# A four-layer trunk on eight cores: reworked order, norms, pooling, convolution, weight layout and tail

## The chip, the cores and the metric

The kernel runs on the 8 cores of one Trainium2 chip, each core on one sequence of the batch, with its own copy of all weights in HBM. The time is the device time of the slowest core in microseconds (us). Cores 0 to 3 and 4 to 7 are the two dies. Some executions fall in a slow state, in which a die shows a lower granted TensorE clock; only fast runs are compared here unless I say otherwise. "Granted clock" is the share of full TensorE clock that the records of a trace show.

## The reference

`x` is (8, 2048, 1024) in FP32. Four layers follow each other; each adds a token mixer and then a squared-ReLU MLP to the residual `x`.

```python
for i in range(4):
    h = rmsnorm(x, norm_mix[i])
    if i % 3 == 0:    # mixer A (layers 0 and 3): gelu(h @ w_in) -> u, v; layernorm(v);
                      # causal mixing of v inside 128 tokens, 8 groups; (u * gate) @ w_out
    elif i % 3 == 1:  # mixer B (layer 1): p = h @ w_in; trailing means over 2, 4, 8, 16 tokens
                      # minus p; a map per group; @ w_out
    else:             # mixer C (layer 2): GLU; causal depthwise conv of 31 taps; layernorm; silu; @ w_out
    x = x + y
    x = x + square(relu(rmsnorm(x, norm_mlp[i]) @ m_w1[i])) @ m_w2[i]      # hidden 4096
return rmsnorm(x, norm_final)
```

## The kernel before

Everything is kept transposed (channels on partitions, `xT`), in four token tiles of 512. Matmuls are BF16 and add up in eight PSUM banks (TensorE's output memory); in this program a bank takes new matmuls only when the engine that reads it is done. Weights come from HBM through a ring of five 1 MB slots and are cast from FP32 to BF16 by the DMA; mixer A loads all its weights once per token tile. A helper records every operation with an estimated cost, and a list scheduler then fixes the order of each engine's instructions from these costs. That order is static: an instruction whose input is late stops everything behind it on its engine.

```python
def c_pool(n=512):                 # the scheduler's estimate for GpSimd
    return 0.15 + n / 500.0

def load_w(src_ap, view, after=()):     # src: rows of a row-major matrix, 512 (or 256) columns wide
    ...
def rms(tt, dst=None):
    # 8x square on ScalarE; 7 sums on GpSimd into sacc/acc; one FP32 matmul with 1/D;
    # sqrt on ScalarE; reciprocal on VectorE
    sum_squares(tt, acc1[:], acc1_r)
    sc.op("pe", MM(bk.v(), onesr[:], acc1[:], True, True), ..., tag="rms")
    sc.op("act", I("activation", out=dst[0], in_=bk.v(), func=AF.Sqrt, ...), table="sqrt")
    sc.op("dve", I("reciprocal", out=dst[0], in_=dst[0]), cost=3.3)

# mixer A, per token tile                        # MLP, per block fb of 512 hidden units and tile
V(tt)            # v = gelu, statistics           W1(i + 1)
ST(tt)           # layernorm of v                 W2(i)   # 8 x (4 matmuls, 1 VectorE add into xT)
self.norm(tt+1)  # norm of the NEXT tile          # after the last block: the next layer's norm
USP(tt)          # u, spatial mixing, gate
WO(tt)           # 24 matmuls, add into xT

# mixer B: window sums by doubling; groups 0..2 on VectorE, group 3 (the longest) on GpSimd
# mixer C: conv taps (128x1536 products) half on VectorE, half on GpSimd
# start: all of x is queued on one DMA queue, the gating weights of mixer A behind it
```

Of the kernel before, what the change touches and what calls it, by code (L numbers as in the profile page):

```python
# [21 lines left out]
CK = 31  # L22

# [142 lines left out]
class Op:  # L166
    __slots__ = ("i", "eng", "fns", "deps", "cost", "dma", "nbytes", "banks", "table", "users", "left",
                 "ready", "start", "end", "pos", "val", "know", "tag")


class Sched:
# [16 lines left out]
    def op(self, eng, fns, rd=(), wr=(), cost=0.1, dma=None, nbytes=0, table=None, after=(), tag=""):  # L188
        if not isinstance(fns, (list, tuple)):
            fns = [fns]  # L190
        o = Op()
        o.i, o.eng, o.fns, o.cost, o.dma, o.nbytes, o.table, o.tag = len(self.ops), eng, fns, cost, dma, nbytes, table, tag
        deps = set(after)
        banks = []
        for r in rd:
            assert not r.dead, tag
            deps |= r.w
        for r in wr:
            assert not r.dead, tag
            deps |= r.used()  # L200
        for r in rd:
            r.r.add(o.i)
        for r in wr:
            r.w = {o.i}
            r.r = set()
            r.subs = []
        for r in list(rd) + list(wr):
            if isinstance(r, Bank) and r not in banks:
                banks.append(r)
                r.refs.append(o.i)  # L210
        deps.discard(o.i)
        o.deps, o.banks = deps, banks
        self.ops.append(o)
        return o.i

    def schedule(self):
# [15 lines left out]
        table = [None]  # L232
        dma_free = 0.0
        bank_avail = {b: (0.0, ()) for b in range(self.NB)}
# [13 lines left out]
        while done < n:  # L248
            best = None
            for e in self.ENGS:  # L250
# [4 lines left out]
                for i in avail[e]:  # L255
# [3 lines left out]
                    if nb:  # L259
# [9 lines left out]
                        if len(fr) < len(nb) or (old >= self.RESERVE and len(fr) < len(nb) + self.RESERVE):  # L269
                            continue  # L270
                        rt = max(rt, fr[len(nb) - 1])
                    cand.append((max(rt, t0), i))
# [25 lines left out]
            free[e] = s + cost  # L298
            if o.dma is not None:
# [20 lines left out]
    def emit(self, block, banks):  # L320
# [52 lines left out]
        def play(eng):  # L373
            def body(e):
                for lst, o in plan[eng]:
                    for k, v in lst:
                        e.wait_ge(sems[k], v)
                    for f in o.fns[:-1]:
# [30 lines left out]
def c_pool(n=512):  # L409
    return 0.15 + n / 500.0  # L410
# [10 lines left out]
def build_program(S, layers, final):  # L421
# [15 lines left out]
    if 0 in kinds:  # L437
        din("a_w_in", (2, D, 2 * AW))
# [3 lines left out]
        din("a_w_out", (2, AW, D))  # L442
    if 1 in kinds:
        din("b_w_in", (1, D, D))
        din("b_w_grpT", (1, 4, 256, 256))
        din("b_w_out", (1, D, D))
    if 2 in kinds:
        assert S == 2048
        din("c_w_in", (1, 4, D, 512))
        din("c_taps", (4, 128, 32 * 48))  # L450
        din("c_b_dw", (D,))
        din("c_w_out", (1, D, D))
        x_spill = nc.dram_tensor("x_spill", [NT, 128, 5, 512], F32, kind="Internal").ap()
    if layers:
        din("m_w1", (4, D, HID))
        din("m_w2", (4, HID, D))
# [4 lines left out]
    uid = [0]  # L461

    def place(name, shape, dt, off, nres):
        uid[0] += 1
        size = int(np.prod(shape[1:])) * DSIZE[dt]
        assert off % 32 == 0 and off + size <= top, (name, off + size - top)
        t = nc.alloc_sbuf_tensor_at(f"{name}_{uid[0]}", list(shape), dt, offset=off)
# [10 lines left out]
    xr = lambda kc, tt: x_r[kc * NT + tt]  # L478
# [7 lines left out]
    onesf, (onesf_res,) = pers("onesf", (128, 128), F32)  # L486
    epst, (eps_res,) = pers("epst", (128, 1), F32)
    sqb = [pers(f"sq{i}", (128, 512), F32) for i in range(NSQ)]
# [14 lines left out]
    ring_n = [0]  # L503

# [5 lines left out]
    def load_w(src_ap, view, after=()):  # L510
        a, b = view
        t, r, key = take_slot()
        dst = t[:, 0:a * b].rearrange("p (a b) -> p a b", a=a)
        sc.op("pool", I("dma_start", out=dst, in_=src_ap, max_dma_last_dim=8192), wr=[r], cost=0.95,
              dma=key, nbytes=128 * a * b * 4, after=after, tag="load")
        return dst, r

    def wmat(name, idx, k0, nk, c0, nc_):

        return dram[name][idx, k0 * 128:(k0 + nk) * 128, c0:c0 + nc_].rearrange("(kc p) f -> p kc f", p=128)  # L520
# [7 lines left out]
    for tt in range(NT):  # L528
        for q in range(4):
            o = sp_dma(f"x{tt}_{q}", xT[:, 2 * q:2 * q + 2, tt * 512:(tt + 1) * 512], dram["x"][tt, :, 2 * q:2 * q + 2, :],  # L530
                       wr=[xr(2 * q, tt), xr(2 * q + 1, tt)], nbytes=128 * 4096, after=first_x[-1:] if tt else ())
            if tt == 0:
                first_x.append(o)
    sc.op("dve", I("memset", onesf[:], 1.0), wr=[onesf_res])
    sc.op("dve", I("tensor_scalar", out=onesr[:], in0=onesf[:], scalar1=1.0 / D, scalar2=None, op0=ALU.mult),
          rd=[onesf_res], wr=[onesr_res])
    sc.op("dve", I("memset", epst[:], EPS), wr=[eps_res])

# [3 lines left out]
    def sum_squares(tt, acc, acc_r):  # L542

        for kc in range(KC):
            if kc == 0:
                sq, sq_r = sacc, sacc_r
            else:
                sq, (sq_r,) = sqb[sqn[0] % NSQ]
                sqn[0] += 1
            sc.op("act", I("activation", out=sq[:], in_=xs(kc, tt), func=AF.Square),  # L550
                  rd=[xr(kc, tt)], wr=[sq_r], cost=c_act(), tag="sq")
            if kc:
                last = kc == KC - 1
                sc.op("pool", I("tensor_tensor", out=acc if last else sacc[:], in0=sacc[:], in1=sq[:], op=ALU.add),
                      rd=[sq_r, sacc_r] if last else [sq_r], wr=[acc_r if last else sacc_r], cost=c_pool(), tag="sqadd")

    def rms(tt, dst=None):

        if dst is None:
            t, (r,) = rsb[rbn[0] % 2]  # L560
            rbn[0] += 1
            dst = (t[:], r)
        sum_squares(tt, acc1[:], acc1_r)
        bk = Bank()
        sc.op("pe", MM(bk.v(), onesr[:], acc1[:], True, True), rd=[acc1_r, onesr_res], wr=[bk], cost=c_pe(1), tag="rms")
        sc.op("act", I("activation", out=dst[0], in_=bk.v(), func=AF.Sqrt, bias=epst[:, 0:1], scale=1.0),
              rd=[bk, eps_res], wr=[dst[1]], cost=c_act(), table="sqrt", tag="rsq")
        sc.op("dve", I("reciprocal", out=dst[0], in_=dst[0]), wr=[dst[1]], cost=3.3, tag="rec")
        return dst

    def rmsnorm(tt, gcol, hT, hr):
        rs, rs_r = rms(tt)
        for kc in range(KC):
            sc.op("dve", I("scalar_tensor_tensor", out=hT[:, kc, :], in0=xs(kc, tt),
                           scalar=pv[:, gcol + kc:gcol + kc + 1], in1=rs, op0=ALU.mult, op1=ALU.mult),
                  rd=[xr(kc, tt), rs_r, pv_res], wr=[hr[kc]], cost=c_dve(), tag="hT")

    def add_to_x(dc, tt, bk):
        sc.op("dve", I("tensor_tensor", out=xs(dc, tt), in0=bk.v(), in1=xs(dc, tt), op=ALU.add),
              rd=[bk], wr=[xr(dc, tt)], cost=c_dve(), tag="xadd")  # L580
# [4 lines left out]
    def mlp(l, after_tile):  # L585
        gcol = PCOLS[f"norm_mlp{l}"]
        hT = [zone(f"mh{tt}", (128, KC, 512), BF16, 8 * KB * tt, KC) for tt in range(NT)]
        aT, rl, rst, w = [], [], [], {}
        n = 8 * NT

        def prep(tt):
            h, hr = hT[tt]
            rst.append(zone(f"mrs{tt}", (128, 512), F32, 46 * KB + 2 * KB * tt))
            for kc in range(KC):
                sc.op("dve", I("tensor_scalar", out=h[:, kc, :], in0=xs(kc, tt), scalar1=pv[:, gcol + kc:gcol + kc + 1],
                               scalar2=None, op0=ALU.mult), rd=[xr(kc, tt), pv_res], wr=[hr[kc]], cost=c_dve(512, 1.4), tag="mh")
            rms(tt, (rst[tt][0][:], rst[tt][1][0]))

        def W1(i):
            fb, tt = divmod(i, NT)  # L600
            if fb == 0:
                prep(tt)
            if i == 0:
                aT.extend(zone(f"aT{j}", (128, 4, 512), BF16, 32 * KB + 4 * KB * j, 4) for j in range(2))
                rl.extend(zone(f"rl{j}", (128, 512), F32, 40 * KB + 2 * KB * j) for j in range(3))
            if tt == 0:
                w[fb] = (load_w(wmat("m_w1", l, 0, 8, fb * 512, 512), (8, 512)),
                         load_w(wmat("m_w2", l, fb * 4, 4, 0, 1024), (4, 1024)))
            wa, wr_ = w[fb][0]
            a, ar = aT[i % 2]  # L610
            h, hr = hT[tt]
            for fc in range(4):
# [3 lines left out]
                r, (rr,) = rl[(i * 4 + fc) % 3]  # L616
# [5 lines left out]
        def W2(i):  # L622
            fb, tt = divmod(i, NT)
            wb, wr_ = w[fb][1]
            a, ar = aT[i % 2]
            for dc in range(KC):
                bk = Bank()
                sc.op("pe", [MM(bk.v(), wb[:, fc, dc * 128:(dc + 1) * 128], a[:, fc, :], fc == 0, fc == 3)
                             for fc in range(4)], rd=[wr_] + ar, wr=[bk], cost=c_pe(4), tag="W2")
                add_to_x(dc, tt, bk)  # L630
            if fb == 7:
                after_tile(tt)

        W1(0)
        for i in range(n):
            if i + 1 < n:
                W1(i + 1)
            W2(i)

    class MixA:  # L640
# [6 lines left out]
        def norm(self, tt):  # L647
            self.h[tt] = mix_h(tt)
            rmsnorm(tt, self.gcol, *self.h[tt])

        def after_tile(self, tt):
            if tt < 2:
# [25 lines left out]
        def body(self, first):  # L678
            ia, h = self.ia, self.h
            if first:  # L680
                self.norm(0)
            v, v_r = zone("a_v", (128, 4, AW), BF16, 0, 24)
            vr = lambda c, vp: v_r[c * 6 + vp]
            bvb, (bv_r,) = zone("a_bvb", (128, AW), BF16, 24 * KB)
            st, st_r = zone("a_st", (128, 4, 6, 6), F32, SM_OFF + 14 * KB, 24)
            sm, sm_r = zone("a_sm", (128, 4, 4), F32, SM_OFF + 14 * KB + 576, 4)
            sc.op("pool", I("dma_start", out=bvb[:], in_=dram["a_bv"][ia].partition_broadcast(128), max_dma_last_dim=8192),
                  wr=[bv_r], cost=0.95, dma=sc.dma_key(f"a_bv{ia}"), nbytes=128 * 4 * AW,
                  after=first_x[-1:] if first else (), tag="bv")

            def V(tt):
                hT, hr = h[tt]
                for vp in range(6):
                    wv, wvr = load_w(wmat("a_w_in", ia, 0, 8, AW + vp * 512, 512), (8, 512),
                                     after=first_x[1:2] if first and tt == 0 else ())
                    for c in range(4):
                        bk = Bank()
                        sc.op("pe", [MM(bk.v(), hT[:, kc, c * 128:(c + 1) * 128], wv[:, kc, :], kc == 0, kc == KC - 1)
# [524 lines left out]
```

## Time and profile before

| | us |
|---|---|
| three runs at first | 3412.93, 3418.42, 3989.4 |
| the profiled execution, by core | 6789.2 to 8748.3 |

The execution that was profiled was slow. These lines are the head of its page and its 40 slices; a digit is a tenth.

```profile
span 8748.3 us, 45371 instructions; the slowest of 8 cores (6789.2 to 8748.3 us)
PE 8645.4 (99%) x15640; PEld 2691.2 (31%) x15640; DVE 2240.3 (26%) x3222; ACT 925.1 (11%) x1460; POOL 645.6 (7%) x572
...
PEclk9999999833333333333333333333333344444444
...
PE 99%; DVE 1%; issue 0%; POOL 0%; DMA 0%; ACT 0%; DVEq 0%; SPq 0%; POOLq 0%; ACTq 0%
```

The page says "TensorE, 99%", which is true of this execution and useless for the change: at a third of the clock TensorE hides every wait. What such a profile still gives are durations of the other engines, counts, and the few gaps that stay open even then. These are the longest waits of TensorE on its fastest core (engine, what it waited for, us in total, times, longest):

```profile
PE bank L159 <- POOL acc_57 L159: 35.7, 3, 24.5
PE bank L159 <- DVE hT_19_61 L159: 15.5, 1, 15.5
PE bank L159 <- DVE c_z_104_147 L159: 15.0, 1, 15.0
PE bank L159 <- DVE c_h_125 L159: 12.2, 1, 12.2
PE bank L159 <- DVE mh_110_153 L159: 5.5, 1, 5.5
```

They point at the start, mixer C and the MLP after it.

### The profile page before, as it was taken

The page shows a single profiled execution, that of the slowest core. Times are in us where ns is not written, and L with a number is a line of the kernel's source. Part 1 is how long each engine was busy: PE and PEld are TensorE (multiplying, and loading weights), DVE is VectorE, ACT ScalarE, POOL GpSimd, SP SyncE. Part 2 cuts the span into 40 slices and gives each one's busy share as a digit, 9 for nine tenths or more (in the row PEclk, how much of TensorE's full clock was granted, in tenths as well). Part 3 has the DMA queues.
Part 4 walks back from the last instruction along what each step waited for, and adds up shares of the span by engine and source line. Part 5 has one row for each costly group of instructions (what it writes and reads, how often), then busy time and mean ns, then how long its engine had stood idle before and what let it go on. Part 6 is the DMA issues. An engine that isn't in the chain of part 4 may idle for free.

```text
span 8748.3 us, 45371 instructions; the slowest of 8 cores (6789.2 to 8748.3 us)
## 1 busy us (share of the span) xinstructions
PE 8645.4 (99%) x15640; PEld 2691.2 (31%) x15640; DVE 2240.3 (26%) x3222; ACT 925.1 (11%) x1460; POOL 645.6 (7%) x572
## 2 busy tenths in 40 slices
PE   8999999999999999999999999999999999999998
PEld 2323232232222222222223432222223233333332
DVE  2212020222222244222223233222232123332224
ACT  1101010110000011100001111000011011110001
POOL 2000000010000022000002101000010011010001
PEclk9999999833333333333333333333333344444444
DMA  5232322230000021000001111000013444430101
GB/s 100 30 46 30 46 34 41 42 50 10 15 15 15 12 44 20 10 15 15 15 7 40 17 34 24 15 15 15 15 23 47 59 63 63 69 47 15 20 15 39
DMA packets 283438, 271.49 MB, mean 31 GB/s; under 512 B 4944, under 2 KB 251856, under 8 KB 283216
## 3 DMA queue, kind: packets, MB, share of 16 engines
q0 software_dynamic: 268144, 238.57, 18.4%
q1 hardware_dynamic: 15072, 30.02, 1.0%
q8 instruction: 133, 2.18, 0.1%
q14 instruction: 89, 0.73, 0.0%
HBM read 493.49 MB, written 13.63 MB: 58 GB/s over the span
## 4 chain that ended last, share of the span: by engine, by line
PE 99%; DVE 1%; issue 0%; POOL 0%; DMA 0%; ACT 0%; DVEq 0%; SPq 0%; POOLq 0%; ACTq 0%
PE bank L159 99%; DVE xT_43 L159 0%; DVE hT_19_61 L159 0%; DVE c_h_125 L159 0%; POOL sacc_56 L159 0%; DVE rs_16_58 L159 0%; POOL c_T_97_140 L159 0%; DMA xT_43<-x 0%; DVE c_z_104_147 L159 0%; DVE rs_17_59 L159 0%; DVE c_st_128 L159 0%; POOL acc_57 L159 0%; DVE mh_110_153 L159 0%; DVE c_mv_129 L159 0%; ACT rs_16_58 L159 0%
## 5 line engine op out<-in xcount | busy, mean ns | idle before, releaser
L159 DVE TENSOR_TENSOR xT_43<-bank,xT_43 128x512 f32<-128x512 f32 x1120 | 772.8, 691 | 2547.3 <-PE bank L159 2547.3
L159 DVE SCALAR_TENSOR_TENSOR bank<-bank,pv_49,a_S_66 128x512 f32<-128x512 f32 x96 | 72.2, 758 | 459.7 <-PE bank L159 459.3
L159 DVE TENSOR_TENSOR bank<-bank,a_bvb_63 128x512 f32<-128x512 f32 x96 | 67.2, 700 | 472.7 <-PE bank L159 463.2
L159 PE MATMUL bank<-a_uT_70,ring_6_48 128*128 128x512 bf16 x192 | 149.1, 1038 | 0.0
L159 PE MATMUL bank<-a_uT_70,ring_4_46 128*128 128x512 bf16 x192 | 148.9, 1038 | 0.0
L159 PE MATMUL bank<-a_uT_70,ring_5_47 128*128 128x512 bf16 x192 | 148.8, 1036 | 0.0
L159 DVE SCALAR_TENSOR_TENSOR bank<-bank,pv_49,a_S_149 128x512 f32<-128x512 f32 x96 | 71.8, 757 | 259.6 <-PE bank L159 259.6
L159 DVE TENSOR_TENSOR bank<-bank,a_bvb_169 128x512 f32<-128x512 f32 x96 | 67.2, 700 | 248.2 <-PE bank L159 248.2
L159 ACT ACTIVATE a_v_62<-bank 128x512 bf16<-128x512 f32 x96 | 56.8, 599 | 659.8 <-DVE bank L159 659.8
L159 ACT ACTIVATE a_uT_70<-bank,pv_49 128x512 bf16<-128x512 f32 x96 | 66.2, 689 | 539.8 <-PE bank L159 539.8
L159 POOL TENSOR_TENSOR sacc_56<-sacc_56,sq_13_55 128x512 f32<-128x512 f32 x72 | 93.3, 1296 | 285.1 <-ACT sq_13_55 L159 267.6
L159 ACT ACTIVATE a_v_168<-bank 128x512 bf16<-128x512 f32 x96 | 57.4, 598 | 479.9 <-DVE bank L159 479.9
L159 POOL TENSOR_TENSOR sacc_56<-sacc_56,sq_11_53 128x512 f32<-128x512 f32 x72 | 93.1, 1292 | 157.4 <-ACT sq_11_53 L159 137.6
L159 ACT ACTIVATE a_uT_172<-bank,pv_49 128x512 bf16<-128x512 f32 x96 | 66.2, 690 | 345.8 <-PE bank L159 345.7
L159 POOL TENSOR_TENSOR sacc_56<-sacc_56,sq_12_54 128x512 f32<-128x512 f32 x72 | 92.5, 1285 | 131.9 <-ACT sq_12_54 L159 96.0
L159 PEld LDWEIGHTS bank<-a_wmb_67,a_v_62 128*128 128x128 bf16 x384 | 71.8, 207 | 92.8 <-issue 88.7
L159 PE MATMUL bank<-a_uT_172,ring_3_45 128*128 128x512 bf16 x192 | 97.5, 720 | 0.0
L159 PE MATMUL bank<-a_uT_172,ring_2_44 128*128 128x512 bf16 x192 | 97.5, 722 | 0.0
L159 PE MATMUL bank<-a_uT_172,ring_6_48 128*128 128x512 bf16 x192 | 97.5, 720 | 0.0
L159 PE MATMUL bank<-a_wmb_67,a_v_62 128*128 128x128 bf16 x384 | 95.0, 461 | 0.0
L159 ACT ACT_TABLE_LOAD x45 | 57.7, 1283 | 327.2 <-PE bank L159 274.0
L159 PE MATMUL bank<-ring_6_48,c_h_125 128*128 128x512 bf16 x128 | 76.4, 833 | 12.2 <-DVE c_h_125 L159 12.2
(805 smaller groups left out, 12835.8 us busy)
## 6 DMA issues: line engine op xcount, KB each, us to landing
ring_2_44<-a_w_in POOLq DMA_DIRECT2D x20, 1024.0 KB, 8.1
ring_3_45<-a_w_in POOLq DMA_DIRECT2D x20, 1024.0 KB, 8.3
ring_4_46<-a_w_in POOLq DMA_DIRECT2D x20, 1024.0 KB, 8.3
ring_5_47<-a_w_in POOLq DMA_DIRECT2D x20, 1024.0 KB, 8.2
ring_6_48<-a_w_in POOLq DMA_DIRECT2D x16, 1024.0 KB, 8.2
ring_4_46<-m_w POOLq DMA_DIRECT2D x14, 1024.0 KB, 8.4
ring_2_44<-m_w POOLq DMA_DIRECT2D x13, 1024.0 KB, 8.3
ring_3_45<-m_w POOLq DMA_DIRECT2D x13, 1024.0 KB, 8.4
```

Of the source, the lines that this page charges most:

```text
L159: return lambda e: getattr(e, _method)(*[_r(a) for a in args], **{k: _r(v) for k, v in kwargs.items()})
```

## The change

Its intent is to take away every wait of TensorE. Its title names four parts (last two MLP blocks added jointly, conv taps built on GpSimd, last conv channels in two parts, tail in three parts), but it reworks all layers. The diff, cut to its core:

```diff
 # scheduler: costs, shared port, bank reservation; activation tables loaded by hand
-    return 0.15 + n / 500.0
+    return 0.2 + n / 400.0
+                    if o.port:      # VectorE and GpSimd not at once on the shared port
+                        rt = max(rt, port_free["pool" if e == "dve" else "dve"])
-                        if len(fr) < len(nb) or (old >= self.RESERVE and len(fr) < len(nb) + self.RESERVE):
+                        if len(fr) < len(nb) + old:
 # weights laid out slot by slot
-        din("a_w_in", (2, D, 2 * AW))
+        din("a_w_in", (2, 12, 128, 4096))       # and all others
 # norms: Ln and Exp on ScalarE in place of Sqrt and reciprocal; sums on GpSimd, VectorE or TensorE
+        if mode == "pe":                        # 8 FP32 matmuls add the squares up
+                sc.op("pe", MM(bk.v(...), onesr[:], sq[:, cs], kc == 0, kc == KC - 1), ...)
+    inv_sqrt: Ln(x + eps), Exp(-0.5 .)
 # start: first matmuls on x * g without the norm; x of later tiles loaded later
+                raw[0] = (hraw, hraw_r)
+                load_x(tt + 1, (cj // 4,), [last_load[0]])
 # mixer A: where the next tile's norm stands
                 ST(tt)
-                if tt + 1 < NT and h[tt + 1] is None:
-                    self.norm(tt + 1)
                 USP(tt)
+                if tt + 1 < NT:
+                    self.norm(tt + 1, after=[late_u[0]])
 # mixer B: all four groups as running sums on VectorE
-                        sc.op(eng, I("tensor_tensor", out=dst..., in0=src..., in1=src[shifted], op=ALU.add), ...)
+                        sc.op("dve", I("tensor_tensor_scan", ..., op0=ALU.add, op1=ALU.subtract), ...)
 # MLP: blocks 6 and 7 in one PSUM accumulation
+                    W2((6, 7), tt)
 # tail: last tile in three column parts
+                    cuts = ((0, 256), (256, 384), (384, 512))
 # mixer C: scaling of x on ScalarE, taps mostly on GpSimd and ahead, last channels in two parts
+                built[(i, j)] = taps(*units[i][j], *cms[Q], "dve" if j % 4 == 3 else "pool")
+            stages = [(0, 0, 256), (1, 0, 256), (2, 0, 256), (3, 0, 128), (3, 128, 128)]
```

## The prediction

> **What bounds the kernel now.** The timed runs (3413, 3418 us, and one of 3989) are not what the profile shows: the profiled execution took 6789 to 8748 us. In it 512-column matmuls start every 0.443 us at best, up to 0.84, also where the windows print a clock of 1.00, so those records are incomplete. TensorE is 98 to 99% of the chain of waits and hides almost everything. The trace counts 14,112 matmuls of 512 columns and 1,408 of 128. At the warm intervals that the Trainium skill states (TensorE: Matmul & The Clock Gate, "Wait — 56ns, not 53.3ns?": 215.7 and 55.6 ns; no run here shows them) I estimate 3,122 us, about 3,145 with the FP32 norm matmuls. That leaves some 275 us of 3418 in which TensorE waits. Only these can go.
>
> **Where they are, by estimate.**
> - Start: first matmul at 40.7 us (chain): x, seven GpSimd adds of 1.27, a 3.35 us reciprocal, eight normed tiles at 1.35. About 40.
> - Tail: the chain's last 26 us hold no matmul; with the sums before it about 35.
> - Mixer A's weights. A packet of 512 B takes 60 ns, 1,024 B 98, 2,048 B 173 (DMA records). One token tile needs 12 MB in 1,024 B and 6 MB in 512 B packets, over 16 engines about 122 us; TensorE at full clock needs 130. Contention and the ring of five buffers should stall each of eight tiles by 5 to 15 us, together with the LayerNorm between V and U. About 90.
> - Mixer B: VectorE. Its sums took 1.26 us alone, 3.0 to 3.3 beside GpSimd's; about 35.
> - Mixer C and the MLP after it: even throttled, TensorE waits 12.2 us on c_h, 15.0 on c_z, 5.5 on mh; unthrottled about 60.
>
> **What the change does.** Weights laid out slot by slot give long packets (from the three times above 22 ns plus 0.074 per byte: 18 MB in some 95 us): DMA leaves the path, −60. Start on unnormalised x: −24. Tail in three parts, squares summed on TensorE: −24. Pooling as scans on VectorE, GpSimd quiet: −25. Mixer C in finer stages: −30. Ln/Exp in place of square root and reciprocal: mostly hidden. Joint last MLP blocks save 96 VectorE additions of 0.69 us, off the path: 0 to −5. Added: FP32 sums of squares on TensorE for some nine tiles, 63 matmuls at 0.86 us at half clock, so about 0.43: +27, partly hidden in waits; scheduling by corrected costs: −5 to −15.
>
> Sum: about −160: **3255 us**, range 3195 to 3325. Faster by over 2%: 0.87; within 2%: 0.10; slower: 0.03.
>
> **What would show each step right.** Packets mostly above 4 KB, DMA share down by a fifth or more; first V matmul near 16 us; last matmul to end under 12 us; no GpSimd sums and no 3 us VectorE sums in mixer B; conv taps on GpSimd at 3.1 us, no wait of TensorE on them; 96 fewer additions into x; more FP32 matmuls. If the profile is throttled again, its span will scarcely change, and only start, tail and mixer C are to be read from it.
>
> **What would make it wrong.** If mixer A was not DMA-bound at full clock, only some 100 us are won (3310). If a denser TensorE draws a lower clock, or fast executions become rare, the gain is lost. If GpSimd taps and VectorE block each other in mixer C, its share is small.

## The result, and the profile after

| us | all runs | fast runs |
|---|---|---|
| before | 3412.93, 3418.42, 3441.86, 3989.4 | the first three |
| after | 3253.8, 3257.32, 3259.36, 3773.51 | the first three |

The ratio of the fast runs is 0.9511, 95% interval 0.9441 to 0.958: 4.9% faster. A ratio here is the mean of one kernel's fast runs over the mean of the other's in the same rounds, so it is not quite the ratio of the medians that are quoted.

The profile after fell in the fast state. First its head, slices, chain, and the same kind of waits as above (the longest of them).

```profile
span 3252.2 us, 46091 instructions; the slowest of 8 cores (3246.7 to 3252.2 us)
PE 3190.4 (98%) x16113; PEld 1533.5 (47%) x16113; DVE 1943.1 (60%) x3053; ACT 967.9 (30%) x1595; POOL 535.7 (16%) x568
...
PEclk9999999999999999999899999999999999999999
...
PE 94%; DMA 2%; issue 1%; DVE 1%; POOL 1%; ACT 0%; SPq 0%; DVEq 0%; POOLq 0%; ACTq 0%
```

```profile
PE bank L161 <- POOL c_acc L161: 14.8, 1, 14.8
PE bank L161 <- DMA a_brow<-a_bv: 3.9, 1, 3.9
PE bank L161 <- DVE a_vv_184 L161: 3.5, 4, 0.9
PE bank L161 <- ACT c_z_163 L161: 3.1, 1, 3.1
```

The waits on VectorE's `hT`, `c_h` and `mh` are gone (1.0 us is left on ScalarE's `c_h`) and that on `c_z` fell to 3.1 us; one long wait is left, on `c_acc`, and it is new. But these lines cannot be set against the throttled ones: a fast profile of the kernel before is needed. That is the first experiment.

### The profile page after: what moved, and what is told of

Same layout as the page of the kernel before. It is cut to its first block, busy times and chain, and to the rows that moved or that the text cites. A ratio compares the mean times of both kernels' runs of the same rounds, so it can differ in the third digit from the quotient of the medians.

```text
span 3252.2 us, 46091 instructions; the slowest of 8 cores (3246.7 to 3252.2 us)
## 1 busy us (share of the span) xinstructions
PE 3190.4 (98%) x16113; PEld 1533.5 (47%) x16113; DVE 1943.1 (60%) x3053; ACT 967.9 (30%) x1595; POOL 535.7 (16%) x568
## 3 DMA queue, kind: packets, MB, share of 16 engines
q0 software_dynamic: 66320, 237.79, 45.3%
## 4 chain that ended last, share of the span: by engine, by line
PE 94%; DMA 2%; issue 1%; DVE 1%; POOL 1%; ACT 0%; SPq 0%; DVEq 0%; POOLq 0%; ACTq 0%
PE bank L161 94%; DMA ring_45<-a_w_in 1%; DMA ring_47<-b_w_out 0%; DMA xT<-x 0%; DMA x_spill<-xT 0%; DVE xT L161 0%; POOL a_smv_187 L161 0%; DVE a_vv_184 L161 0%; POOL a_sm L161 0%; POOL sacc L161 0%; DVE a_v L161 0%; DVE a_S L161 0%; POOL ring_47 L161 0%; POOL c_ls L161 0%; DVE b_w_111 L161 0%
## 5 line engine op out<-in xcount | busy, mean ns | idle before, releaser
L161 DVE TENSOR_TENSOR xT<-bank,xT 128x512 f32<-128x512 f32 (+2 forms) x1040 | 706.5, 683 | 481.6 <-PE bank L161 471.4
L161 ACT ACTIVATE a_uTv_188<-bank,pv 128x512 bf16<-128x512 f32 x96 | 65.9, 686 | 100.5 <-PE bank L161 100.4
L161 ACT ACTIVATE a_uT<-bank,pv 128x512 bf16<-128x512 f32 x96 | 65.3, 686 | 100.0 <-PE bank L161 96.9
L161 DVE SCALAR_TENSOR_TENSOR bank<-bank,pv,a_Sv_165 128x512 f32<-128x512 f32 x96 | 72.0, 758 | 27.0 <-PE bank L161 26.8
L161 DVE SCALAR_TENSOR_TENSOR bank<-bank,pv,a_S 128x512 f32<-128x512 f32 x96 | 71.7, 757 | 24.8 <-PE bank L161 24.6
L161 DVE BATCH_NORM_STATS2 a_stv_186<-a_vv_184 128x6 f32<-128x512 bf16 x96 | 65.6, 687 | 25.3 <-ACT a_vv_184 L161 25.3
L161 POOL TENSOR_TENSOR sacc<-sacc,sq_57 128x512 f32<-128x512 f32 x52 | 66.8, 1284 | 80.4 <-ACT sq_57 L161 71.6
L161 DVE TENSOR_TENSOR bank<-bank,a_bvbv_185 128x512 f32<-128x512 f32 x96 | 66.1, 688 | 17.8 <-PE bank L161 17.8
L161 POOL TENSOR_TENSOR sacc<-sacc,sq_59 128x512 f32<-128x512 f32 x52 | 66.0, 1270 | 61.6 <-ACT sq_59 L161 52.4
L161 POOL TENSOR_TENSOR sacc<-sacc,sq_55 128x512 f32<-128x512 f32 x52 | 66.0, 1270 | 56.0 <-ACT sq_55 L161 45.1
L161 DVE TENSOR_TENSOR a_uTv_188<-bank,a_uTv_188 128x512 bf16<-128x512 f32 x96 | 65.5, 690 | 12.6 <-DVE bank L161 12.3
L161 ACT ACTIVATE sq_57<-xT 128x512 f32<-128x512 f32 x64 | 40.0, 625 | 45.3 <-POOL sacc L161 30.3
L161 ACT ACTIVATE sq_59<-xT 128x512 f32<-128x512 f32 x63 | 39.4, 625 | 36.1 <-POOL sacc L161 20.5
```

Of the source, the lines that this page charges most:

```text
L161: return lambda e: getattr(e, _method)(*[_r(a) for a in args], **{k: _r(v) for k, v in kwargs.items()})
```

## The experiments

Two theories of where the gain came from. Theory 1 is the prediction's largest term: mixer A was bound by its weights, and longer packets freed it. Theory 2 is order: engines ran their instructions in an order made from wrong costs, so TensorE waited on VectorE and GpSimd; a better order and shorter chains removed that. A third theory came up on the way, about a wait that the change itself made.

The changed kernel was not timed again in the later jobs. Experiments on it are compared with it by their ratios to the kernel before, and by the spans and stages of their fast profiles. The jobs resolve some 5 us, not less. The edits below are cut to their main lines; a comment in them can stand for lines left out.

### The kernel before, profiled (no edit)

> The kernel before, unchanged, for a profile in the fast state, which the first profile was not. Expected: about 3420 us; 512-column matmuls every 0.2155 us as in the profile after; TensorE waits some 250 us in all. Theory 1 (weights bound mixer A): the largest waits of TensorE are on weight DMAs in the two mixer A layers, and a token tile takes 138 us or more there against 131 after. Rival (order and chains): TensorE in mixer A waits on VectorE and ScalarE between V and U, hardly on a DMA.

Two of its three runs were slow (3585.37, 3983.01); the fast one took 3414.24 us and was profiled.

```profile
span 3411.0 us, 45371 instructions; the slowest of 8 cores (3402.7 to 3411.0 us)
PE 3184.2 (93%) x15640; PEld 1479.7 (43%) x15640; DVE 2227.7 (65%) x3222; ACT 914.7 (27%) x1460; POOL 664.5 (19%) x572
```

```profile
PE bank L159 <- POOL acc L159: 44.7, 9, 24.7
PE bank L159 <- DVE xT L159: 25.6, 8, 6.8
PE bank L159 <- DVE hT L159: 23.2, 2, 15.2
PE bank L159 <- ACT a_v L159: 21.8, 1, 21.8
PE bank L159 <- DVE c_h L159: 20.3, 1, 20.3
PE bank L159 <- DVE b_pl L159: 19.7, 3, 13.2
PE bank L159 <- DVE c_z L159: 16.7, 2, 15.0
PE bank L159 <- DVE mh L159: 10.6, 2, 6.5
```

TensorE is busy 3184 us before and 3190 after: the change took no work off it. All gaps of TensorE over 0.2 us sum to a median of 206.2 us per core before and 53.5 after, a difference of 152.7 us, against 155.7 in span. And not one line names a weight DMA, on any core. That speaks against theory 1 already. (In the changed kernel a few short ones appear: 2.4 to 5.9 us per core on `a_w_in`.)

To see where, I cut each core's trace at the last matmul of every stage. The table gives medians over the undisturbed cores, in us; its columns are computed from the traces. In the order and norm columns the kernel before is edited, as below.

| stage | before | before, new order | before, late norm | before, late x and scans | after |
|---|---|---|---|---|---|
| to the first matmul of V | 40.6 | 38.5 | 35.4 | 35.3 | 17.2 |
| mixer A, layer 0, tile 0 | 156.8 | 163.1 | 159.7 | 139.2 | 141.7 |
| tiles 1 to 3 | 131.2, 134.7, 131.2 | 131.2 each | 132.9, 132.9, 131.4 | 134.3, 142.0, 131.2 | 131.0, 131.0, 130.7 |
| MLP 0 | 456.6 | 448.0 | 457.6 | 457.6 | 443.9 |
| mixer B | 167.3 | 167.1 | 166.6 | 141.4 | 132.1 |
| MLP 1 | 441.2 | 443.3 | 441.2 | 441.2 | 443.4 |
| mixer C to its first output matmul | 198.4 | 192.8 | 195.6 | 198.8 | 174.7 |
| mixer C, output | 64.5 | 65.9 | 65.3 | 65.8 | 65.7 |
| MLP 2 | 458.5 | 462.1 | 457.4 | 458.2 | 452.5 |
| mixer A, layer 3, four tiles | 542.0 | 524.8 | 530.1 | 542.8 | 523.7 |
| MLP 3 | 454.6 | 448.0 | 454.8 | 454.6 | 451.5 |
| tail | 28.2 | 35.0 | 28.1 | 28.7 | 11.3 |
| span | 3406.2 | 3383.2 | 3389.0 | 3371.8 | 3250.5 |

Most of mixer A's tiles were already at 131 us before. Nothing about the weights held them. What did hold the others is in the trace. This is VectorE in the kernel before at the end of MLP 0 (start, us, instruction; waits in brackets), where the norm of the next layer is due:

```profile
1040.52 3.33 DVE L159 RECIPROCAL rs<-rs 128x512 f32<-128x512 f32 x1
1043.78 0.62 DVE L159 TENSOR_TENSOR xT<-bank,xT 128x512 f32<-128x512 f32 x1
1044.32 9.16 DVE L159 SCALAR_TENSOR_TENSOR hT<-xT,pv,rs 128x512 bf16<-128x512 f32 x8
1053.41 5.46 DVE L159 TENSOR_TENSOR xT<-bank,xT 128x512 f32<-128x512 f32 x9
```

```profile
1038.64 8.81 PE L159 MATMUL bank<-aT,ring 128*128 128x512 bf16 x40
1054.24 1.86 PE L159 MATMUL bank<-aT,ring 128*128 128x512 bf16 x4 [6.79 <-DVE xT L159]
```

The reciprocal and eight norm steps keep VectorE for 12.5 us, the additions that would free PSUM banks stand behind them, and TensorE stops for 6.79 us with work at hand. Part of that length comes from GpSimd: its sums of squares run beside these eight steps (9.16 us), while eight of the same steps from 1019.92 us on, with GpSimd idle, took 5.38 us. In mixer A the same block (a reciprocal and 10.43 us of `hT`) stood between two gate steps. At the end of MLP 0 in the changed kernel TensorE has no gap, and it is VectorE that waits:

```profile
993.96 1.89 PE L161 MATMUL bank<-aT_87,ring_44 128*128 128x512 bf16 x8
995.10 0.69 DVE L161 TENSOR_TENSOR xT<-bank,xT 128x512 f32<-128x512 f32 x1 [1.90 <-PE bank L161]
```

### The layout of the weights alone, in both directions

Before with the new layout (taps and C's input matrix left as they were):

```diff
-        return dram[name][idx, k0 * 128:(k0 + nk) * 128, c0:c0 + nc_].rearrange("(kc p) f -> p kc f", p=128)
+        return dram[name][idx, blk]        # (128, 4096) per slot, contiguous per partition
```

> The kernel before with nothing changed but the weights of mixer A, B's and C's matrices and the MLPs laid out slot by slot in HBM (taps and C's input matrix left). Theory 1: 50 to 90 us faster than before (about 3350), packets of 3 to 4 KB in place of 0.5 and 1 KB. Rival: within 15 us of before, since HBM rather than packets sets the rate, or TensorE did not wait for weights.

Its fast runs took 3424.95 and 3448.05 us (two slow ones 3750 and 3751): not faster. The packets changed as wanted (4,096 B and 3,072 B in place of 1,024 and 512), mixer A's tiles did not (131.2, 134.4, 131.2 us). Only tile 0 moved, and for the worse, from 156.8 to 178.8 us: TensorE waited 35.1 to 40.7 us by core, not 12.6 to 22.1, behind the gating weights. (The start before it fell by 5 us.)

After with the old layout (taps and C's input matrix again left as they were, so their layout is tested by neither run):

```diff
-            last_load[0] = sc.op("pool", I("dma_start", out=t[:, i * n:(i + 1) * n], in_=dram[name][idx, blk, :, i * n:(i + 1) * n],
+            src = dram[name][idx, k0 * 128:(k0 + ka) * 128, cb * b:(cb + 1) * b].rearrange("(kc p) f -> p kc f", p=128)
```

> The changed kernel with the row-major weights of before (packets of 0.5 and 1 KB), all else kept. Theory 1: 50 to 90 us slower than the changed kernel (about 3320 to 3340), lost in mixer A as waits on weight DMAs. Rival: within 15 us of it.

Four fast runs, 3259.71 to 3265.62 us; ratio to the kernel before 0.9539 (0.9494 to 0.9584), where the changed kernel had 0.9511. Its median span is 3253.9 against 3250.5 us. The layout is worth some 3 to 5 us, at the edge of what the jobs resolve and an order less than the 60 foretold. Theory 1 falls.

The reason is in the stretch from 210 to 470 us, two tiles of mixer A. The last three figures are clock, DMA share (the mean of 16 engines' busy time) and GB/s. First the changed kernel with the old layout, then the changed kernel:

```profile
210.00:470.00 260.00, 256.63 (x1329) 121.95 (x1329) 158.86 (x237) 86.72 (x136) 77.40 (x80) 1.00 1.18 160
```

```profile
210.00:470.00 260.00, 258.21 (x1336) 122.52 (x1334) 160.38 (x239) 88.07 (x138) 70.67 (x83) 1.00 0.99 159
```

Both move the same 160 GB/s, what TensorE asks for, although the short packets fill 1.18 of the engines' time. A share above 1 means that packets overlap. The Trainium skill says so of descriptors in one queue of one engine (DMA: Bandwidth & Descriptors, "Two DMAs through the same engine are not ordered": they start in order but are pipelined), and this share agrees. So my sum of packet times, 122 us for a tile of 130, was no bound at all.

### Additions of the last two MLP blocks, one after the other

```diff
+                W2((6,), tt)
-                    W2((6, 7), tt)
+                    W2((7,), tt)
```

> The changed kernel with the last two MLP blocks added to x one after the other, in the same order of matmuls by block: 96 additions of 0.69 us more on VectorE, the same matmuls. Theory (off the path): 0 to 8 us slower. Rival (VectorE holds up TensorE at the ends of the MLPs, where the norms of the next layer also run): 20 us or more slower.

Fast runs 3252.3 and 3253.54 us (two slow ones), ratio 0.9511 (0.9441 to 0.9582), the same as the changed kernel's. VectorE works 2003.8 us in place of 1943.1, and no stage grew by over 3 us. The joint additions gain nothing that these runs can see.

### Order alone: the kernel before with the changed scheduler

```diff
-    return 0.15 + n / 500.0
+    return 0.2 + n / 400.0
+        o.port = (eng == "pool" and dma is None) or (eng == "dve" and tag in PORT)
+                    if o.port:
+                        rt = max(rt, port_free["pool" if e == "dve" else "dve"])
-                        if len(fr) < len(nb) or (old >= self.RESERVE and len(fr) < len(nb) + self.RESERVE):
+                        if len(fr) < len(nb) + old:
```

> The kernel before with the same instructions, only ordered by the changed scheduler: GpSimd costed at 1.48 us for a 128x512 sum in place of 1.17 (the trace shows 1.28 to 1.48 from start to start), the shared port of VectorE and GpSimd modelled, and the changed rule for bank reservation. Theory 2 (order): the waits of TensorE on GpSimd's sums of squares and on additions into x at the ends of MLP 0, 2 and 3 (11.5, 11 and 10 us of gaps) shrink; 15 to 40 us faster than before. Rival (the chains themselves are too long, whatever the order): within 10 us of before.

Four fast runs (one slow), 3387.25 to 3391.44 us, ratio 0.9927 (0.9911 to 0.9942): 25 us from order alone, with the same instructions. All of mixer A's tiles but the first fall to 131.2 us (3.5 us in layer 0, 17 in layer 3), MLP 0 and MLP 3 by 8.6 and 6.6 us; the tail loses 7 of that again, and tile 0 six.

### The next tile's norm placed later, in mixer A alone

```diff
                 ST(tt)
-                if tt + 1 < NT and h[tt + 1] is None:
-                    self.norm(tt + 1)
                 USP(tt)
+                if tt + 1 < NT:
+                    self.norm(tt + 1, after=[late_u[0]])
```

> The kernel before with one thing moved: in mixer A the norm of the next token tile is issued after the spatial gating (and waits for the sixth U block), not between V and the gating, and only tile 0 is normed at the end of an MLP. Theory 2: the first A layer's tile 2 and the second's tiles 4 to 6 fall from 134.7, 139.7, 136.0 and 134.7 us to about 131; 10 to 20 us faster than before. Rival: the tiles stay, because what delays the gating is the LayerNorm chain with its table load and square root; within 5 us.

Three fast runs (one slow), 3395.14, 3397.09 and 3398.88 us, ratio 0.9953 (0.9931 to 0.9974): 16 us. The four tiles of layer 3 fall from 542.0 to 530.1 us, each to about 132.9, not 131. So this placement and the new order are two ways to the same 12 to 17 us; with right costs the scheduler found it without the move.

### Later loads of x, and mixer B by scans

```diff
-    # all of x queued at once; gating weights behind it
+                    load_x(tt + 1, range(4), [last_load[0]])      # tile by tile, gating weights first
-                        sc.op(eng, I("tensor_tensor", ...), tag="padd")        # doubling sums
+                        sc.op("dve", I("tensor_tensor_scan", ...), tag="scan")
```

> The kernel before with two changes in stages that do not touch: (a) token tiles 1 to 3 of x are loaded tile by tile, and the loads of the gating weights come before them, not behind all of x; (b) mixer B's window sums as VectorE scans, without GpSimd. Theory: (a) removes the 21.8 us wait of TensorE at 57 to 79 us (a gelu queued in ScalarE behind a copy that waits for the gating weights), so the first tile falls from 161.8 to about 142 us after the first matmul; (b) mixer B falls from 167.5 to 135 to 145 us. Together 40 to 55 us faster than before. Rival for (b): VectorE itself is the limit, and the scans cost as much; mixer B over 158 us.

Four fast runs, 3374.96 to 3401.19 us, ratio 0.9924 (0.9882 to 0.9967), a little less than expected; the two slower ones had two cores at a clock of 0.97 where the others had 0.977. The stages part the two effects. (a) Tile 0 falls from 156.8 to 139.2 us. In the kernel before its gap looked like this (matmuls, and ScalarE at the same time):

```profile
40.67 16.22 PE L159 MATMUL bank<-ring,hT 128*128 128x512 bf16 x64 [15.21 <-DVE hT L159]
78.66 3.75 PE L159 MATMUL bank<-a_ws,onesf 128*128 128x512 f32 x4 [21.76 <-ACT a_v L159]
```

```profile
75.54 1.06 ACT L159 ACTIVATE a_wmb<-a_ws 128x1024 bf16<-128x1024 f32 x1 [11.47 <-POOL a_ws L159]
76.62 1.28 ACT L159 ACT_TABLE_LOAD   x1
77.91 2.56 ACT L159 ACTIVATE a_v<-bank 128x512 bf16<-128x512 f32 x5
```

ScalarE stood at a copy of the gating weights, which had landed behind all of `x`, with five gelus queued after it; PSUM filled up. But tile 1 rose from 131.2 to 134.3 and tile 2 from 134.7 to 142.0, so 10 us of the win were given back. (b) Mixer B falls from 167.3 to 141.4 us. Its sums before and the scans after, on VectorE (mean ns of one):

```profile
L159 DVE TENSOR_TENSOR b_t<-b_t 128x1050 f32<-128x1050 f32 x8 | 15.7, 1958 | 0.4
L159 DVE TENSOR_TENSOR b_t<-b_t 128x1042 f32<-128x1042 f32 x4 | 8.8, 2210 | 0.3
```

```profile
L161 DVE TENSOR_TENSOR_SCAN b_w_113<-b_px_107,b_ca 128x512 f32<-128x512 f32 x4 | 5.1, 1275 | 1.0 <-ACT b_px_107 L161 1.0
```

Single sums of these two sizes took from 1.23 to 3.41 us in that trace, the longest while GpSimd ran sums of its own. This agrees with the Trainium skill (SBUF — State Buffer, "SBUF: two separate sides"), which calls the port pair that VectorE and GpSimd share an exclusive lock, not a split of bandwidth. In the changed kernel a scan that carries a sum on takes 1.26 to 1.28 us for 512 elements per partition, so per element it is only half as fast as an uncontended sum. Fewer passes therefore saved VectorE nothing: its 24 window sums took 42.0 us before, the 32 scans 44.9 us in this run. What went is GpSimd's part, 16 sums of 36.4 us for the longest window, and with it the longer VectorE steps beside them (the step that makes `b_pl`: 28.2 us before, 22.0 here). TensorE's waits on `b_pl` fell from 19.7 us to 7.6.

### The changed kernel in the order of wrong costs

```diff
-    return 0.2 + n / 400.0
+    return 0.15 + n / 500.0
-                    if o.port:
-                        rt = max(rt, port_free["pool" if e == "dve" else "dve"])
-                      ..., cost=3.3 if eng == "pool" else c_dve(1536, 1.8), port=True, tag="cT")
+                      ..., cost=c_pool(1536) if eng == "pool" else c_dve(1536), port=True, tag="cT")
```

> The changed kernel, same instructions, ordered with the costs of before for GpSimd (1.17 us for a 128x512 sum, 3.2 for taps as before) and without the model of the shared port. Theory 2 (order is worth much): 15 to 40 us slower than the changed kernel. Rival (the new chains leave slack, so the order hardly matters): within 8 us.

Three fast runs (three slow), 3269.04 to 3273.62 us, ratio 0.9584 (0.9567 to 0.9601); span 3266.8 against 3250.5: 16 us slower. Ten of these are in mixer C (174.7 to 184.4), the rest about 1 us in most tiles of mixer A and 1 to 2 in three of the MLPs. Theory 2 holds, from both sides, for 16 to 25 us. The two edits are not exact opposites: here the rule for bank reservation stays, and the cost of the taps is wrong too.

### Taps half on VectorE, and an undivided tail

```diff
-                built[(i, j)] = taps(*units[i][j], *cms[Q], "dve" if j % 4 == 3 else "pool")
+                built[(i, j)] = taps(*units[i][j], *cms[Q], "pool" if j // 2 % 2 else "dve")
-                if last and tt == NT - 1:
+                if False:
```

> The changed kernel with two parts undone in stages that do not touch: (a) conv taps half on VectorE and half on GpSimd (pairs in turn), as before, in place of three quarters on GpSimd; (b) the last token tile added, normed and stored whole, in place of 256, 128 and 128 columns. Theory: (a) is worth little, mixer C (from the end of MLP 1 to its first output matmul, 174.7 us) moves by less than 4 us either way, and may even fall, since in the changed kernel TensorE waits 14.8 us on GpSimd while it builds taps; rival: taps on GpSimd are what shortened mixer C, which rises by 10 us or more. (b) the tail after the last matmul of the MLP grows from 11 to 15 to 20 us.

Six of its seven runs were slow, one die at 0.83 to 0.96; the fast one took 3243.71 us, so no ratio was given. The stages come from the undisturbed die of the profiled run. (a) Mixer C falls from 174.7 to 168.5 us: moving taps to GpSimd costs the changed kernel 6 us. It is the wait on `c_acc` that shrinks, from 14.3 to 16.7 us by core to 8.8 to 10.8, the same wait that the run with later taps removes below; so the two gains must not be added. (b) The tail grows from 11.3 to 15.2 us, but MLP 3 falls from 451.5 to 445.5, so the two together go from 462.8 to 460.7. The division in three gains nothing; it moves time from one stage to the other. What shortened the end against the kernel before (482.8 us for both) is kept in this run: squares summed on TensorE, and Ln and Exp, which take 0.61 to 0.69 us each, in place of the 3.35 us reciprocal. Which of these two does more was not measured.

### The last conv channels in one part

```diff
-            stages = [(0, 0, 256), (1, 0, 256), (2, 0, 256), (3, 0, 128), (3, 128, 128)]
+            stages = [(0, 0, 256), (1, 0, 256), (2, 0, 256), (3, 0, 256)]
```

> The changed kernel with the last 256 channels of the convolution in one part, not two of 128: all their taps, transposes, convolutions and statistics come after the last input matmul. Theory: mixer C up to its first output matmul grows by 8 to 15 us (four more transposes, four more conv blocks of 0.7 us and up to 18 us of taps on GpSimd are exposed). Rival: within 3 us, since taps can be built ahead and TensorE has other work.

Four fast runs, 3252.07 to 3255.0 us, ratio 0.9526 (0.9508 to 0.9545); mixer C takes 173.7 us in place of 174.7. The rival was right: dividing the channels is worth nothing here.

### Taps later

Mixer C's one long wait in the changed kernel, 14.84 us on `c_acc` (14.3 to 16.7 by core), is new. This is GpSimd in that wait, in the changed kernel:

```profile
1576.42 3.10 POOL L161 TENSOR_TENSOR c_T_154<-ring_44,c_mask 128x1536 bf16<-128x1536 bf16 x1
...
1582.72 0.16 POOL L161 MEMSET c_yT<- 128x64 bf16 x1 [0.53 <-DMA x_spill<-xT]
1582.84 1.27 POOL L161 TENSOR_TENSOR sacc<-sacc,sq_55 128x512 f32<-128x512 f32 x1
1584.07 3.08 POOL L161 TENSOR_TENSOR c_T_152<-ring_44,c_mask 128x1536 bf16<-128x1536 bf16 x1
1587.10 1.97 POOL L161 TENSOR_TENSOR sacc<-sacc,sq_57 128x512 f32<-128x512 f32 x1
1589.04 3.07 POOL L161 TENSOR_TENSOR c_T_153<-ring_44,c_mask 128x1536 bf16<-128x1536 bf16 x1
...
1597.72 1.26 POOL L161 TENSOR_TENSOR c_acc<-sacc,sq_57 128x512 fp32r<-128x512 f32 x1
```

Taps (`c_T`), which nobody needs for another 30 us, stand between the sums (`sacc`) that everybody waits for. The profile blames the sum.

```diff
-                built[(i, j)] = taps(*units[i][j], *cms[Q], "dve" if j % 4 == 3 else "pool")
+                built[(i, j)] = taps(*units[i][j], *cms[Q], "dve" if j % 4 == 3 else "pool",
+                                     [self.acc_done] if i == 0 else ())
```

> The changed kernel with one dependence more: the taps of the first 256 channels are not built before the last sum of squares for mixer C is done. In the changed kernel five tap builds of 3.08 us on GpSimd stand between those sums while TensorE waits 14.8 us on the last. Theory 3 (the taps on GpSimd hold up the sums): that wait falls to under 5 us, mixer C from 174.7 to about 163 us, the kernel 9 to 13 us faster than the changed one. Rival (the wait comes from the spill of x, which a GpSimd memset waits for, or from ScalarE's squares): the wait stays above 10 us.

Three fast runs, 3240.93, 3242.58 and 3246.76 us (two slow ones), ratio 0.9498 (0.9476 to 0.9519). Mixer C takes 163.0 us, and the wait (2.6 to 6.0 us by core) is on one of them:

```profile
PE bank L161 <- POOL c_acc L161: 4.4, 1, 4.4
```

Theory 3 holds, with the size that was expected. On this core GpSimd idles 3.99 us before the memset, which waits for the spill of x; that seems to be what is left of the wait, and was not tested.

### Taps later, and the last sums on VectorE

```diff
+            self.acc_done = sum_squares(tt, ..., "dve" if tt == NT - 1 else "pool")
```

> As the run with late taps, and the sums of squares of the last token tile before mixer C on VectorE (0.69 us each) in place of GpSimd (1.48 us from start to start). Expected: the wait of TensorE at the start of mixer C nearly gone, 12 to 17 us faster than the changed kernel, about 3242 us; the fastest of all. If VectorE, which also adds the MLP into x there, is held up by ScalarE's squares, it gains nothing over late taps alone.

Three of six runs were slow. The fast ones took 3236.88, 3237.33 and 3240.5 us, ratio 0.9483 (0.9461 to 0.9504); the changed kernel's best was 3253.8. On the undisturbed die mixer C takes 158.2 us and the median span is 3232.0, against 174.7 and 3250.5. The line for `c_acc` reads, on one of its cores:

```profile
PE bank L161 <- DVE c_acc L161: 0.2, 1, 0.2
```

This version beats both kernels, by some 18 us against the changed one. Those two were not timed in one job, and their ratio intervals overlap (the changed kernel's, 0.9441 to 0.958, is wide); but their fast runs are 13 us apart at the nearest. Taps half on VectorE on top of it was not run.

## Why the prediction was right or wrong

The time was right: 3255 was foretold, the fast runs took 3253.8 to 3259.36. That it came so close is luck: the sum was right for partly wrong reasons, and the step that failed was its largest.

- **"Mixer A's weights ... DMA leaves the path, −60": failed.** The layout alone gave no gain in the kernel before and 3 to 5 us in the changed one. The mistake was to add up packet times as if an engine ran one packet after the other; the trace shows a share of 1.18. TensorE's waits in mixer A were not on the large weights: before, it had no wait on a weight DMA, and what held tile 0 was the late copy of the small gating weights on ScalarE. Mixer A did gain, 15.1 us in tile 0, 4.4 in tiles 1 to 3 and 18.3 in layer 3, 37.8 in all, but by the order of the loads of `x` and of the norms. The symptom was guessed, its cause was not.
- **"Start on unnormalised x: −24": right.** The first matmul of V came at 17.2 in place of 40.6 us, −23.4. The prediction said "near 16". No experiment undid it; the start is read from the two traces. Three edits of the kernel before (new layout, late norm, late x) shortened the start by 5 us without it, so some of the 23.4 may not be its doing.
- **"Pooling as scans, GpSimd quiet: −25": right for that part.** The scans gave 25.9 us by themselves; mixer B as a whole fell by 35.2. The other 9 us were not taken apart.
- **"Mixer C in finer stages: −30": the size is near, the cause is wrong.** Mixer C lost 22.5 us (262.9 to 240.4), MLP 2 another 6. But the finer last part gained 1 us at most, and taps on GpSimd cost 6. What went are the waits on `c_h` (20.3 us; that scaling now runs on ScalarE) and on `c_z` (15.0 to 3.1); those two are argued from the traces. The forecast "no wait of TensorE on taps" was met in name only: the taps held up the sums, for 14.8 us.
- **"Tail in three parts, squares summed on TensorE: −24": size right, half of the cause wrong.** MLP 3 and tail fell from 482.8 to 462.8, −20; the three parts have no share in it.
- **"FP32 sums on TensorE, +27": right.** 95 FP32 matmuls of 512 columns in place of 40 in the two traces, at some 0.425 us from start to start, make 23 us; a few narrower ones come on top.
- **"Joint last blocks: 0 to −5": right**, no gain seen.
- **"Scheduling, −5 to −15": too small.** Order alone gave 25 us in the kernel before, and taking it back cost 16 in the changed one. The ends of MLP 0 (−12.7) and MLP 3 were not in my list at all.
- **"DMA share down by a fifth": failed.** Fast against fast, the packets of the weight queue took 50.0% before and 45.3% after.
- **The estimate of 275 us of waits** was a little too high: 206 us of gaps and 15 us after the last matmul. Matmuls at a slow clock after the pauses cost some 26 us before and 11 after, counted from the intervals over 0.3 us.
- **"If a denser TensorE draws a lower clock": it did not.** In the fast profiles the mean granted clock was 0.976 to 0.977 before and 0.991 to 0.994 after. One of four timed runs of the changed kernel was slow, and 8 of 28 of the kernel before; four runs are too few to say whether fast executions became rarer.

So two errors met: −60 that did not come, and 37.8 in mixer A plus 12.7 in MLP 0 and more in B that came unforeseen. A right total is no proof of its terms. Not all of the gain is shown by experiment either: edits of the kernel before gave 23 us (order) and 34 us (later loads of x with scans) of the 155.7 us in span, each by itself. The start, mixer C and the end, 66 us together, are read from the traces.

## What to carry to other kernels

When instructions are put in order ahead of time, a wrong cost for a slow helper engine can put its work in front of what frees the busiest engine; here that was worth 16 to 25 us. Look for urgent work queued behind work that can wait, and add the one dependence that forbids it. Do not sum packet durations into a bandwidth bound; ask the trace whether TensorE ever waits on that DMA. And get a profile in the state that you want to explain, before explaining it.

## What the Trainium skill lacked or had wrong

- TensorE: Matmul & The Clock Gate, "Seeing it yourself", says that dense matmuls on a third core of a die bring the whole die to 13/16 of the clock within 5 to 20 us, and to budget 1.95 GHz for all-core work. Here all eight cores ran dense matmuls for 3250 us at a mean granted clock of 0.991 to 0.994, and start to start was 215 to 216 ns. Some runs of the same kernels did show a die at 0.81 to 0.84 (0.809 to 0.816 in one of 3983.01 us), others at 0.91 or 0.96, and the first profile had 512-column intervals of mostly 443 to 840 ns. The page's condition, a third busy core, held in every run alike, so it does not tell when which state comes, and these runs don't settle it.
- The same page, "Wait — 56ns, not 53.3ns?", gives 215.7 and 55.6 ns; the fast traces agree (215 to 216, 55 to 56). It has no interval for the FP32 matmuls used here (a single matmul on operands read as float32r, which the trace prints as f32): 512 columns took 418 to 430 ns from start to start, about twice as long as BF16.
- DMA: Bandwidth & Descriptors has no figure for how far packets overlap: 512 and 1,024 B packets, 60 and 98 ns at the median, sustained the same 160 GB/s of BF16 as packets of 3,072 and 4,096 B, at a share of 1.18 against 0.99.
- DVE: opcode table, instruction layouts, handler registers and perf-mode slots, "6. Datapath and trigger behaviour", says that the built-in running sum goes at half throughput, without a duration. The traces agree: 128x512 in FP32 took 1.26 to 1.28 us, an addition of that size 0.69 us.
